# The first group's output projection as Strassen pairs: branches added in attention, one k pair's operands formed there, two up pairs' weights formed beside the queries

## The chip, the cores and the metric

The kernel runs on one NeuronCore of a Trainium2 chip. The metric is the device time of one execution in microseconds. In the views, PE is the tensor engine (PEld its weight loads), DVE the vector engine, ACT the scalar engine, POOL the GpSimd engine and SP the engine whose queue issues most DMAs.

## The reference

One layer of a decoder for 1024 prompt positions and 8 samples of 8 positions, D = 1024, all fp32. What matters here, for each group of tokens:

```python
q, k, v, gu, gv, ga, gb = split_in(rmsnorm(x, norm_mix) @ w_in)
o = sink_attention(q, k, v, ...)                # window of 128, 16 heads of 64
s = spatial_gating(gelu(gu), layernorm(gelu(gv)), ws, bs)
merged = sigmoid(ga) * (o @ w_pa) + sigmoid(gb) * (s @ w_pb)
x = x + merged @ w_out                          # the output projection
f, nconv = conv_ffn(rmsnorm(x, norm_ffn), w_up, conv_w, conv_b, w_down, conv_prev)
return rmsnorm(x + f), ...
```

`merged @ w_out` is 1088 tokens by 1024 by 1024. Also returned are the windows of keys and values, the last convolution rows and the normalised v rows of the samples.

## The kernel before

**Layout.** Activations are kept transposed: a tile holds 128 features on the partitions and tokens along the columns. D is KD = 8 such tiles. The tokens are two groups: group 0 has 576 columns (64 sample and 512 prompt tokens), group 1 has 512.

**Precision.** An fp32 product is made of three products in fp32r. `split` writes a high part with a cast on ACT and the remainder with a subtraction on DVE (L40, L41); a product of weights w and activations x is then `wh·xh + wh·xl + wl·xh`. So each weight tile and each operand costs a cast on ACT and a subtraction on DVE before PE can use it.

**Two kinds of product.** `mm3` (L239) is the ordinary one: for an output tile, 8 k tiles times 3 products, in two column chunks (320 and 256 for group 0). `Chain` makes two output tiles together from two halves of the columns by the Strassen-Winograd scheme: 7 products instead of 8, each of 4 k pairs times 3 matmuls of half a group's columns (288 or 256). Its weights are seven combinations, four of them sums on DVE (`Weights.total`, L178), each split by itself. Its operands are seven combinations per k pair: `combine` (L261 to L264) makes four of them with four DVE instructions of 288 columns, and `split` then runs over all seven. The results of the seven products are put together from PSUM: `keep` copies some to SBUF on ACT (L280 to L282), and additions on DVE and one subtraction on POOL combine them (`put`, L287).

**Weights.** `Weights` (object `W`) has a list of units, one for each split. `W.get(ahead, loads)` returns the next unit's pair of tiles, and emits the splits of `ahead` units and the loads of `loads` items beyond it. Raw weights have 4 buffers and split ones 4 slots.

**Order.** The program is written as one order of Python calls; each engine runs its own instructions in the order that a scheduler of the framework gives them, and waits on semaphores. SP's queue issues the DMAs in its order. Long stages take a list of small jobs between their products: `behind(at, j)` runs one after each product of the first Strassen stage, `fill` after each step of attention.

**Stages**, with the times of the profile: normalisation and the first projections (0 to 112 us), Strassen pairs for queries, keys, gates and the gated unit (to 462; the queries of both groups run from about 133 to 222), attention of group 0 with the branch products `branch` between its steps (465 to 585), attention of group 1 with group 0's merge between its steps (585 to 681), the rest of group 1's merge (to 715.3), the output projection of group 0 (to 766.9) and group 1 (to 813), the up projection with the convolution (to 1273), the down projection and the end.

**Merge.** `merge(g, c, to)` multiplies the attention's output by w_branch_attn for tile c and multiplies the result by the gate (L1099). For group 1 it adds the stored branch product too (L1101). For group 0 the gated product is stored to DRAM (`msd`). In the stage of group 1's merge, `hold` loads product and branch of group 0's tile c again, they are added (L1402), and `operand` splits the sum into a plain operand of 576 columns.

**Output projection.** Group 0's eight tiles are `mm3` products. The addition of x is made from PSUM (L1418), the result is stored to `x1d`, squared on ACT (L1421, L1427), and the squares are summed on POOL (L1428).

**Up pairs formed early.** For the first NPRE = 2 pairs of up tiles, `pair_load`, `pair_unit` and `store` form the seven units from raw weights (sums at L1376), split them and store high and low parts to DRAM (`upd`). They are 16 steps: 4 run in group 1's merge, 12 in the output projection of group 0. The up projection loads them later as ready weights.

## Time and profile before

| | |
|---|---|
| Runs | 1518.04, 1520.92, 1520.64 us; median 1520.64 us |
| Profiled execution | 1520.02 us, span 1518.1 us, granted clock 0.997 |
| Query stage, 133 to 222 us | 89.0 us |
| Attention of group 1, 585 to 681 us | 96 us |
| Rest of group 1's merge | 681.0 to 715.3 us |
| Output projection of group 0 | 715.3 to 766.9 us |
| Output projection of group 1 | 766.9 to 813.0 us |

In a row of the window table each engine has its busy time in the window and the number of its instructions; PEclk is the granted clock of the tensor engine as a share of full speed. In a timeline a row is one instruction: start, duration, engine, line, operation, names of output and inputs, shapes, and in brackets how long the engine had been idle and what released it. Matmuls overlap, so their price is the distance of their starts and not their duration. A row of the waits reads: engine, name and line of the waiting instruction, what it waited for, total us, times, longest. A group of equal instructions has its busy time and mean ns behind the bar, and then the idle time of the engine before them.

### The profile page before, as it was taken

To read this page: it belongs to the slowest core of one execution; us is meant where nothing else is said; L and a number is where in the kernel's file an instruction comes from. 1 tells how busy PE (TensorE), PEld (TensorE's weight loads), DVE (VectorE), ACT (ScalarE), POOL (GpSimd) and SP (SyncE) were. 2 spreads that over 40 slices of the span, in tenths; PEclk is the share of its full clock that TensorE was granted. 3 is DMA by queue.
4 is the path that set the end of the run, shared out by engine and by line. 5 is a ranking of instruction groups with operands and counts; after the bars stand their busy time and mean duration, and the time that the engine had idled before them with its cause. 6 is when DMAs were issued, how large, how long until landed. Compare 5 with 4: busy or idle time off the path is not lost.

```text
span 1518.1 us, 31397 instructions
## 1 busy us (share of the span) xinstructions
PE 1499.2 (99%) x12194; PEld 1485.4 (98%) x12194; DVE 1158.3 (76%) x1903; ACT 823.3 (54%) x1751; POOL 264.5 (17%) x422
## 2 busy tenths in 40 slices
PE   9999999999999999999999999999999999999998
PEld 9999999999998999999999999999999999999997
DVE  6896778756645895989668888898898888785685
ACT  6655764454543774864444555555555556353463
POOL 0000012200120231330232222232142122000002
PEclk9999999999999999999999999999999999999998
DMA  8553457747759847748988333332332317973353
GB/s 283 165 182 111 178 180 252 233 135 260 241 187 317 269 159 224 235 165 301 338 280 280 128 109 126 114 119 106 107 126 106 107 58 245 361 234 96 117 187 132
DMA packets 137509, 286.70 MB, mean 189 GB/s; under 512 B 15249, under 2 KB 44369, under 8 KB 137361
## 3 DMA queue, kind: packets, MB, share of 16 engines
q1 hardware_dynamic: 132352, 279.85, 55.1%
q10 hardware_dynamic: 5008, 4.85, 0.9%
q8 instruction: 96, 1.57, 0.4%
q14 instruction: 53, 0.43, 0.1%
HBM read 195.76 MB, written 90.85 MB: 189 GB/s over the span
## 4 chain that ended last, share of the span: by engine, by line
PE 68%; DVE 5%; DMA 4%; issue 3%; ACT 2%; SPq 1%; POOL 1%; POOLq 0%; ACTq 0%; DVEq 0%
PE st L299 39%; PE dn L1739 13%; PE mm L239 10%; PE sc L1232 1%; PE pt L1265 1%; ACT s L1255 1%; PE mx L841 1%; DVE wl L41 1%; PE po L1293 1%; DMA sg1d<-z 1%; DMA q<-qd 1%; DMA upd<-hl 0%; DMA s<-sd 0%; POOL x L1800 0%; DMA stg<-mbd 0%
## 5 line engine op out<-in xcount | busy, mean ns | idle before, releaser
L299 PE MATMUL st<-th,wh 128*128 128x256 f32 (+1 forms) x2128 | 610.4, 287 | 2.5 <-ACT k L280 2.3
L299 PE MATMUL st<-tl,wh 128*128 128x256 f32 (+1 forms) x2128 | 608.5, 286 | 0.0
L299 PE MATMUL st<-th,wl 128*128 128x256 f32 (+1 forms) x2128 | 608.1, 286 | 0.0
L299 PEld LDWEIGHTS st<-th,wh 128*128 128x128 f32 x2128 | 400.0, 188 | 4.1 <-ACT k L280 3.4
L299 PEld LDWEIGHTS st<-th,wl 128*128 128x128 f32 x2128 | 400.2, 188 | 0.0
L299 PEld LDWEIGHTS st<-tl,wh 128*128 128x128 f32 x2128 | 399.7, 188 | 0.0
L41 DVE TENSOR_TENSOR wl<-wraw,wh 128x512 fp32r<-128x512 f32 (+2 forms) x204 | 158.8, 791 | 35.3 <-ACT wh L40 33.4
L40 ACT CAST wh<-wraw 128x512 fp32r<-128x512 f32 (+2 forms) x204 | 139.2, 694 | 82.2 <-PE st L299 33.2
L1739 PE MATMUL dn<-th,wh 128*128 128x288 f32 (+1 forms) x616 | 177.3, 288 | 0.0
L1739 PE MATMUL dn<-tl,wh 128*128 128x288 f32 (+1 forms) x616 | 176.8, 287 | 0.0
L1739 PE MATMUL dn<-th,wl 128*128 128x288 f32 (+1 forms) x616 | 176.7, 287 | 0.0
L40 ACT CAST wh<-ws 128x512 fp32r<-128x512 f32 x160 | 98.2, 622 | 101.6 <-PE st L299 63.9
L41 DVE TENSOR_TENSOR wl<-ws,wh 128x512 fp32r<-128x512 f32 x160 | 111.1, 707 | 45.3 <-ACT wh L40 43.3
L1739 PEld LDWEIGHTS dn<-th,wh 128*128 128x128 f32 x616 | 116.7, 190 | 0.0
L1739 PEld LDWEIGHTS dn<-tl,wh 128*128 128x128 f32 x616 | 115.6, 188 | 0.0
L1739 PEld LDWEIGHTS dn<-th,wl 128*128 128x128 f32 x616 | 115.6, 188 | 0.0
L287 POOL TENSOR_TENSOR z<-kn,k 128x256 f32<-128x256 f32 (+1 forms) x32 | 29.6, 931 | 307.5 <-ACT kn L282 290.2
L40 ACT CAST th<-traw 128x544 fp32r<-128x544 f32 (+1 forms) x85 | 54.1, 643 | 52.8 <-PE dn L1739 40.0
L41 DVE TENSOR_TENSOR tl<-traw,th 128x544 fp32r<-128x544 f32 (+1 forms) x85 | 61.4, 730 | 22.9 <-ACT th L40 22.8
L239 PE MATMUL mm<-s,wh 128*128 128x256 f32 (+1 forms) x384 | 76.4, 294 | 0.0
L530 PE MATMUL st<-w2h,th 128*128 128x256 f32 x308 | 74.3, 282 | 0.8 <-ACT w2h L40 0.8
L239 PE MATMUL mm<-ol,wh 128*128 128x256 f32 (+1 forms) x256 | 73.6, 288 | 0.4 <-DVE ol L41 0.4
(298 smaller groups left out, 3156.1 us busy)
## 6 DMA issues: line engine op xcount, KB each, us to landing
wraw<-wt SPq DMA_DIRECT2D x133, 512.0 KB
traw<-td SPq DMA_DIRECT2D x77, 272.0 KB
td<-za SPq DMA_DIRECT2D x22, 544.0 KB
wraw<-wt SPq DMA_DIRECT2D x35, 256.0 KB
upd<-hl SPq DMA_DIRECT2D x14, 512.0 KB
td<-t SPq DMA_DIRECT2D x11, 544.0 KB
qd<-q SPq DMA_DIRECT2D x8, 576.0 KB
q<-qd SPq DMA_DIRECT2D x8, 576.0 KB
```

Source lines behind the costliest of these rows:

```text
L40: S.copy(hi, src)
L41: V.tensor_sub(lo, src, hi.bitcast(F32))
L239: PE.matmul(ps[:, lo:lo + c1 - c0], u[:, k, :], v[:, c0:c1], start=(clear and k == 0 and i == 0), stop=(k == nk - 1 and i == 2), skip_grou ...
L287: op(to, pick(x, to, lo, hi), pick(y, to, lo, hi))
L299: PE.matmul(ps, u[:, kk, :], v, start=first and kk + i == 0, stop=kk == 3 and i == 2, skip_group_check=True)
L530: PE.matmul(ps, u, v[:, k, :], start=k + i == 0, stop=k == KD - 1 and i == 2)
L841: PE.matmul(ps[:, P * i:P * i + P], vn[:, i], late["wst"][:, c, :], start=True, stop=True)
L1232: PE.matmul(ps[:, h, o0:256], q, kst[kv][:, e, k0:cur + P], start=e == 0, stop=e == 1)
L1255: S.activation(s[:, h], s[:, h], AF.Exp, bias=nm[:, h:h + 1], accum_out=dn[:, h:h + 1])
L1265: PE.transpose(pt[:, h * P:h * P + P], s[:, h, 0:P], ident)
L1293: PE.matmul(half(po, e), v[:, b - 1 + e], half(x, e), start=e == 0 and x is ph, stop=False, skip_group_check=True)
L1739: PE.matmul(place(m, e), u[:, m, :], v[:, lo:hi], start=new and i + k == 0 and (e == 0 or m % 2 == 0), stop=i == NU - 1 and k == 2, skip_g ...
```

## The change

**Group 0's output projection is made of four Strassen pairs** (tiles p and p + 4) by a new class `Out(Chain)`: 4 x 7 products of 12 matmuls of 288 columns in place of eight `mm3` tiles. The results are added straight into the two tiles of x: four half tiles per pair by POOL from `keep`'s copies (L1488, L1491), three by DVE from PSUM (L1494). `x1_out` stores, squares and sums as before (POOL's sum is L1477). The weights are units of pairs, with sums and seven splits of 512 in place of two splits of 1024. PSUM has four banks for these products (`psw`), which the output projection of group 1 uses as well.

**The merge of group 0** adds the branch at once, like group 1's (L1147 in both cases), so the eight branches are loaded during the merge of group 0. It runs in the order 0, 4, 1, 5, 2, 6, 3, 7, and tiles 0 and 4 are not stored but kept: they make k pair 0, whose sums and splits run inside attention of group 1. The other six are stored to `msd`, loaded again in the stage of group 1's merge and formed there as k pairs 1 to 3 (`form_sums`, `form_first`, `form_rest`), in place of the loads, additions and plain splits of eight tiles.

**The two up pairs' units** are formed by `up_units`: 16 steps with other loads (12 of 256 KB in place of 4 of 512 KB), the same 14 splits and stores. They run in `behind`, after every second product from the second pair on, beside the queries.

The diff, cut to its core:

```diff
-            for at in (PA0, PA0, WO0, WO0):
-                for c in range(8):
-                    W.add(wt(at + c), KD)
+            for c in (*crossed, *range(8)):
+                W.add(wt(PA0 + c), KD)
+            for c in range(4):
+                W.add_pair(wt(WO0 + c), wt(WO0 + c + 4))
+            for c in range(8):
+                W.add(wt(WO0 + c), KD)
...
+                def step(f, j, x, add, drop):
+                    def go():
+                        if hold:
+                            nc.sync.dma_start(*hold.pop())
+                        if loads:
+                            load(*loads.pop(0))
+                        src = q[x][0]
+                        if add:
+                            V.tensor_add(src, src, q["y"][0])
+                        t = pool.tile([P, 2, 4, P], F32R, name="phl", bufs=2)
+                        split(t[:, 0], t[:, 1], src)
+                        hold.append((upd[f][j], t.bitcast(F32)))
...
             def behind(at, j):
 
+                if ahead and at > 0 and (7 * at + j) % 2 == 0:
+                    with tc.issue_after(W.last.ins), tc.issue_after(W.did[0].ins), tc.issue_after(W.did[1].ins):
+                        ahead.pop(0)()
...
                             V.tensor_mul(st["t"], st["t"], st["ps"][:, base:base + n])
-                            if g:
-                                V.tensor_add(st["t"], st["t"], st["u"])
+                            V.tensor_add(st["t"], st["t"], st["u"])
                             to(c, st["t"])
...
-            keep = lambda c, t: nc.sync.dma_start(msd[c], t)
+            def keep(c, t):
+                if c % 4:
+                    nc.sync.dma_start(msd[c], t)
+                else:
+                    held[c] = t
+                    if c:
+                        form_sums(0, tma, 1)
+                        form_first(0, tma)
+                        form_rest(0)
...
-                    if at == 1:
-                        t, u = held.pop(c)
-                        V.tensor_add(t, t, u)
-                        operand(0)(c, t)
-                        hold(c + 2)
+                    if kk < 4 and at == 0:
+                        if c % 2 == 0:
+                            form_sums(kk, hbp, 2)
+                        else:
+                            form_rest(kk)
                     go()
-                    if at == 2 and c % 2:
-                        ahead.pop(0)()
+                    if kk < 4 and at == 1 and c % 2 == 0:
+                        form_first(kk, tm0)
+                        hold(c + 6)
+                        hold(c + 7)
...
+            class Out(Chain):
+
+                def product(self, j, w):
+                    ps, (xc, xd), n2 = self.multiply(j, w), self.places, self.n2
+                    c0, c1, d0, d1 = (x[:, n2 * h:n2 * h + n2] for x in (xc, xd) for h in range(2))
+                    kept = self.kept
+                    if j in (0, 1, 2):
+                        name, to, op = (("1", c0, G.tensor_add), ("5", d1, G.tensor_sub), ("u", c1, G.tensor_add))[j]
+                        self.keep(name, ps)
+                        op(to, to, kept[name])
+                    elif j == 4:
+                        self.keep("n", ps)
+                        G.tensor_sub(d1, d1, kept["n"])
+                    else:
+                        to, op = {3: (c1, V.tensor_add), 5: (c0, V.tensor_add), 6: (d0, V.tensor_sub)}[j]
+                        op(to, to, ps)
...
-            for c in range(KD):
-                xt = x_next(0, c)
-                w, ps = W.get(), acc2()
-                mm3(ps, groups[0]["chunks"], w, ms[0], 0, KD, KD)
-                for _ in range(1 + c % 2):
-                    ahead.pop(0)()
-                x1_tile(groups[0], c, ps, xt)
+            for p in range(4):
+                xc, xd = xs
+                chain = Out(0, tx, psw, xsp, (xc, xd))
+                for j in range(7):
+                    chain.product(j, W.get(3, 1))
+                    if j == 1 and p < 3:
+                        xs = [x_of(groups[0], c) for c in (p + 1, p + 5)]
+                    if j == 5:
+                        x1_out(0, p, xc)
+                x1_out(0, p + 4, xd)
```

How DVE's order changes late in the attention of group 1, around the end of a block (`of`, `ol` are the block's output, `pl` the low part of its transposed probabilities, `s` the scores, `stg` a merged tile, `wl` the low part of a weight tile). Before:

```order
L1304 TENSOR_TENSOR of_8900<-po_8891,ot_8898 64x256
L41 TENSOR_TENSOR pl_8911<-pt_8905,ph_8910 128x512
L1099 TENSOR_TENSOR stg_8955<-stg_8955,mm_8963 128x576
L41 TENSOR_TENSOR ol2_8576<-of_8900,oh2_8575 128x2x128
L1257 RECIPROCAL dn_8919<-dn_8919 128x4
L41 TENSOR_TENSOR wl_9365<-wraw_9151,wh_9364 128x1024
L1258 TENSOR_TENSOR s_8885<-s_8885,dn_8919 128x4x128
```

Now, at the block with the corresponding merge:

```order
L1350 TENSOR_TENSOR of_8959<-po_8950,ot_8957 64x256 x2
L40 TENSOR_TENSOR pl_8901<-pt_8895,ph_8900 128x512
L1147 TENSOR_TENSOR stg_8858<-stg_8858,stg_8860 128x576
L1303 RECIPROCAL dn_8909<-dn_8909 128x4
L1304 TENSOR_TENSOR s_8852<-s_8852,dn_8909 128x4x128
L1288 COPY_PREDICATED s_8932<-c_mprev_473,sc_8916 128x4x128
L40 TENSOR_TENSOR ol2_8696<-of_8959,oh2_8695 128x2x128
```

The addition of the branch, L1147, now stands between the probabilities' split and the softmax product, and the block's output split stands behind both.

DVE in the output projection of group 0 (`ml7` is the last merge operand, `hl` an up pair's unit, `wl` the low part of this projection's weights, `stg` a tile of x). Before, from the last merge operand on:

```order
L41 TENSOR_TENSOR ml7_9884<-stg_9811,mh7_9883 128x512
L41 TENSOR_TENSOR hl_10020<-ra_9414,hl_10020 128x512
L1418 TENSOR_TENSOR stg_9888<-stg_9888,mm_9898 128x576
L41 TENSOR_TENSOR wl_10099<-wraw_9958,wh_10098 128x1024
L41 TENSOR_TENSOR hl_10086<-rb_9416,hl_10086 128x512
L1418 TENSOR_TENSOR stg_9890<-stg_9890,mm_9964 128x576
L41 TENSOR_TENSOR wl_10169<-wraw_10030,wh_10168 128x1024
L1418 TENSOR_TENSOR stg_9956<-stg_9956,mm_10036 128x576
```

Now, most of the first pair (`ws` is a sum of weights, `st` a bank of PSUM; the names of raw tiles differ only by their buffers):

```order
L177 TENSOR_TENSOR ws_10149<-ws_10122,wraw_9921 128x512
L40 TENSOR_TENSOR wl_10101<-ws_10122,wh_10100 128x512
L177 TENSOR_TENSOR ws_10169<-wraw_9921,wraw_9923 128x512
L1494 TENSOR_TENSOR stg_10003<-stg_10003,st_10029 128x288
L40 TENSOR_TENSOR wl_10148<-ws_10149,wh_10147 128x512
L40 TENSOR_TENSOR wl_10148<-ws_10169,wh_10147 128x512
L177 TENSOR_TENSOR ws_10246<-wraw_10145 128x512
L177 TENSOR_TENSOR ws_10270<-ws_10246,wraw_10143 128x512
L1494 TENSOR_TENSOR stg_10003<-stg_10003,st_10106 128x288
L40 TENSOR_TENSOR wl_10194<-wraw_9921,wh_10193 128x512
L40 TENSOR_TENSOR wl_10194<-wraw_9923,wh_10193 128x512
L1494 TENSOR_TENSOR stg_10005<-stg_10005,st_10007 128x288
```

The additions L1494 from PSUM are shorter and stand among sums and splits of the weights; the up pairs' splits are gone from here.

POOL in the same stage (`rs0` is the sum of squares). Before, one addition for each tile but the first:

```order
L1428 TENSOR_TENSOR rs0_216<-rs0_216,stg_10025 128x576
L1428 TENSOR_TENSOR rs0_216<-rs0_216,stg_10091 128x576
L1428 TENSOR_TENSOR rs0_216<-rs0_216,stg_10161 128x576
L1428 TENSOR_TENSOR rs0_216<-rs0_216,stg_10229 128x576
L1428 TENSOR_TENSOR rs0_216<-rs0_216,stg_10303 128x576
```

Now, the first pair and part of the second:

```order
L1488 TENSOR_TENSOR stg_10003<-stg_10003,k1_10020 128x288
L1488 TENSOR_TENSOR stg_10005<-stg_10005,k5_10042 128x288
L1488 TENSOR_TENSOR stg_10003<-stg_10003,ku_10063 128x288
L1491 TENSOR_TENSOR stg_10005<-stg_10005,kn_10097 128x288
L1477 TENSOR_TENSOR rs0_216<-rs0_216,sq_10140 128x576
L1488 TENSOR_TENSOR stg_10045<-stg_10045,k1_10166 128x288
```

Four additions into the tiles of x precede the square's addition in each pair.

More of the change, by code (lines that the diff above doesn't have):

```diff
@@ L403, in dest256 @@
                 return ready, go
+            crossed = [c + 4 * e for c in range(4) for e in range(2)]
             blocks = {"gv0": GV0, "gv1": GV0 + 2, "gv2": GV0 + 4, "v": V0}
@@ L991, in layer @@
                 if at == 6:
+                    while ahead:
+                        ahead.pop(0)()
                     qko.close()
@@ L1382, in store @@
-            def store():
-                if "store" in pair:
-                    nc.sync.dma_start(*pair.pop("store"))
-            held = {}
-            def hold(c):
-                if c < KD:
-                    held[c] = [pwp.tile([P, 576], F32, name=x, bufs=3) for x in "mb"]
-                    for x, src in zip(held[c], (msd[c], mbd[0][c])):
-                        nc.sync.dma_start(x, src)
-            hold(0)
-            hold(1)
-            ahead = [x for f in range(NPRE) for x in (pair_load(f), *(pair_unit(f, j) for j in range(7)))]
@@ L1397, in layer @@
[L1397 to L1407 removed]
+            pso.close()
@@ L1421, in x1_tile @@
                     S.activation(nacc, x, AF.Square)
[L1422 removed]
+                elif g and c == KD - 1:
                     late["sq"] = traw()[:, :n]
```

147 lines of the change are left out of this document (85 added, 62 removed).

## The prediction

> **What bounds the kernel now.** I read the page first, for the engines' shares.
>
> ```profile
> span 1518.1 us, 31397 instructions
> PE 1499.2 (99%) x12194; PEld 1485.4 (98%) x12194; DVE 1158.3 (76%) x1903; ACT 823.3 (54%) x1751; POOL 264.5 (17%) x422
> ```
>
> The matmul engine works in 99% of the span. A change can gain only by giving it fewer or shorter matmuls, and it loses wherever the matmuls come to wait. The profiled execution took 1520.0 us, 1.9 us more than its span and 0.6 us less than the median of the runs, 1520.64, whose spread is 2.9 us; I sum against 1520.0. The share of DVE, 76%, is a mean over stages, so the second view is the table of busy time by window: the query stage (133 to 222 us), the opening and the middle of the second attention (595 to 672), the rest of the second group's merge (681 to 715), the first group's output projection (to 767) and the first of the up projection.
>
> ```profile
> core 0: us, PE busy (x) PEld busy (x) DVE busy (x) ACT busy (x) POOL busy (x), PEclk, DMA share, GB/s
> 133.00:222.00 89.00, 89.00 (x720) 89.00 (x720) 63.31 (x98) 59.87 (x121) 6.89 (x8) 1.00 0.46 161
> 595.00:606.00 11.00, 11.00 (x87) 10.59 (x86) 8.73 (x14) 7.50 (x26) 2.50 (x8) 1.00 1.08 288
> 606.00:672.00 66.00, 65.73 (x513) 63.57 (x512) 62.18 (x117) 52.95 (x166) 27.08 (x65) 1.00 0.64 204
> 681.00:715.30 34.30, 34.30 (x305) 34.30 (x305) 32.60 (x47) 17.35 (x24) 0.00 (x0) 1.00 0.84 284
> 715.30:766.90 51.60, 51.30 (x390) 51.13 (x389) 32.23 (x39) 20.41 (x29) 10.83 (x8) 1.00 0.94 329
> 813.00:850.00 37.00, 36.91 (x282) 36.71 (x282) 32.44 (x69) 20.16 (x45) 7.05 (x8) 1.00 0.65 228
> ```
>
> PE never rests for long, and the granted clock (PEclk) is full. What differs is DVE: 63.3 of 89 us in the query stage, 62.2 of 66 in the middle of attention, 32.2 of 51.6 in the output projection. So the output projection is bound by matmuls alone, with 19 us of DVE to spare, and attention is the stage in which work handed to DVE has 3.8 us of room. The waits from 681 to 767 us and one piece of the chain say the same:
>
> ```profile
> ACT hl L40 <- DMA upd<-hl: 8.7, 4, 4.2
> PE mm L239 <- DVE stg L1418: 0.3, 1, 0.3
> 718.82 7.39 DMA upd<-hl
> ```
>
> PE waits there once, 0.3 us, for the addition L1418. Behind that stands the store of the up pairs' weights: the casts of the next ones waited 8.7 us for it, and the chain passes through it. After the change those stores are made some 500 us earlier.
>
> **Output projection of the first group, matmuls.** Before, each of the 8 tiles takes 8 k tiles of 3 products in two chunks, 320 and 256 columns: 192 matmuls of each width. The timeline of PE at the stage's first and last matmuls:
>
> ```profile
> 715.29 0.30 PE L239 MATMUL mm<-mh,wh 128*128 128x320 f32 x1
> 715.43 0.31 PE L239 MATMUL mm<-ml,wh 128*128 128x320 f32 x1
> 765.78 0.28 PE L239 MATMUL mm<-mh,wh 128*128 128x256 f32 x1
> 765.90 0.28 PE L239 MATMUL mm<-ml,wh 128*128 128x256 f32 x1
> ```
>
> Records overlap, so the price is the distance of starts, 0.14 to 0.15 and 0.12 us. The stage itself, 51.6 us by its window, holds 192 x 0.147 + 192 x 0.118 = 50.9 and the 0.3 of waiting. After it come 4 pairs x 7 products x 4 k pairs x 3 = 336 matmuls of 288 columns. Such matmuls run in the up projection; the timeline there, two rows ten matmuls apart, and the groups of the window 829 to 846:
>
> ```profile
> 835.83 0.29 PE L299 MATMUL st<-tl,wh 128*128 128x288 f32 x1
> ...
> 837.16 0.29 PE L299 MATMUL st<-th,wl 128*128 128x288 f32 x1
> ...
> L299 PE MATMUL st<-th,wl 128*128 128x288 f32 x44 | 12.9, 294 | 0.0
> L299 PE MATMUL st<-tl,wh 128*128 128x288 f32 x43 | 12.7, 295 | 0.0
> L299 PE MATMUL st<-th,wh 128*128 128x288 f32 x43 | 12.7, 295 | 0.0
> ```
>
> Ten starts in 1.33 us are 0.133; 130 matmuls in 17 us are 0.131. At 0.132 the stage takes 336 x 0.132 = 44.4 us: 51.6 - 44.4 = **7.2 us less**, if nothing stalls. That term is counts by pitches and I hold it for certain.
>
> **The same stage on DVE and POOL.** DVE's price is also a distance of starts. The timeline at 681 us:
>
> ```profile
> 681.38 0.69 DVE L1099 TENSOR_TENSOR stg<-stg,mm 128x512 f32<-128x512 f32 x1 [0.94 <-PE mm L239]
> 681.98 0.75 DVE L1402 TENSOR_TENSOR m<-m,b 128x576 f32<-128x576 f32 x1
> 682.65 0.68 DVE L1101 TENSOR_TENSOR stg<-stg 128x512 f32<-128x512 f32 x1
> ```
>
> So 512 columns cost 0.60 us and 576 cost 0.67; a record reads 0.08 more. A pair's weights need 4 sums and 7 splits of 512: 11 x 0.60 = 6.6 us. Three half tiles of 288 are added from PSUM, at 288/512 of 0.60 some 0.35 each, 1.1 together. That is 7.7 of the pair's 84 x 0.132 = 11.1 us, so DVE alone fits. POOL gets four additions of half a tile (L1488, L1491) and two of the squares (L1477) per pair. Their prices, by POOL's and DVE's timeline near 847 us and the group of the squares:
>
> ```profile
> 824.46 0.81 POOL L287 TENSOR_TENSOR zb<-kn,k 128x288 f32<-128x288 f32 x1 [6.90 <-ACT kn L282]
> 846.93 2.64 POOL L287 TENSOR_TENSOR zb<-kn,k 128x288 f32<-128x288 f32 x1 [5.03 <-ACT kn L282]
> ...
> 847.61 0.68 DVE L178 TENSOR_TENSOR ws<-ws,wraw 128x512 f32<-128x512 f32 x1
> 848.22 0.68 DVE L41 TENSOR_TENSOR wl<-ws,wh 128x512 fp32r<-128x512 f32 x1
> 848.82 0.51 DVE L287 TENSOR_TENSOR za<-k,st 128x64 f32<-128x64 f32 x2
> 849.25 0.87 DVE L41 TENSOR_TENSOR wl<-ws,wh 128x512 fp32r<-128x512 f32 x1
> ...
> L1428 POOL TENSOR_TENSOR rs<-rs,stg x7: 1491/1611/2134, 731.8 to 768.3; 128x576 f32<-128x576 f32 x7
> ```
>
> The same addition takes 0.81 us where DVE leaves it alone and 2.64 where DVE runs sums and splits back to back. It ends at 849.57, after DVE's addition from PSUM at 848.82, and the DVE split that starts beside its end takes 0.87 instead of 0.68. So the two engines do delay one another. Per pair POOL needs 4 x 0.81 + 2 x 1.49 = 6.2 us. The low end of what this costs PE is 0: three such additions lie in 813 to 850, where DVE is as dense, and PE lost 0.09 of 37 us. The high end is that the two never overlap: 6.6 + 6.2 = 12.8 us for a pair of 11.1, so 4 x 1.7 = 6.8 us. DVE's waits for PE and its additions from PSUM leave openings, 4.5 us in each pair; I take a third, **2.3 us more**.
>
> The Trainium skill, page "SBUF — State Buffer", section "Who interferes with whom", says that a DVE instruction with two SBUF inputs and a GpSimd instruction that reads SBUF exclude one another for their whole length, while a DVE instruction with at most one SBUF input does not. By that rule this term would be the high end and the forecast some 4.5 us later. The 2.64 us row agrees with it, the 0.09 us that PE lost does not yet decide.
>
> **Second attention.** Each of the 8 merges of the first group now adds its branch there (L1147): 8 x 0.67 = 5.4 us on DVE. The first k pair's operands are formed there too. The groups of the same work, done for the up projection between 772 and 850 us:
>
> ```profile
> L41 DVE TENSOR_TENSOR tl<-t,th 128x1152 fp32r<-128x1152 f32 x4 | 5.4, 1351 | 0.0
> L41 DVE TENSOR_TENSOR tl<-x,th 128x576 fp32r<-128x576 f32 x4 | 3.0, 749 | 0.0
> L261 DVE TENSOR_TENSOR t<-x 128x288 f32<-128x288 f32 x4 | 2.9, 718 | 0.0
> L264 DVE SCALAR_TENSOR_TENSOR t<-t,x 128x288 f32<-128x288 f32 x4 | 1.8, 449 | 0.0
> L41 DVE TENSOR_TENSOR tl<-x,th 128x288 fp32r<-128x288 f32 x4 | 1.8, 448 | 0.0
> ```
>
> One k pair: two sums at 0.72, two at 0.45, splits of 0.45, 0.75 and 1.35, together 4.9, and 7 x 0.08 of overlap less: 4.3 us. Ends: 0, if DVE's room and PE's merge matmuls cover all; 5.4 + 4.3 = 9.7, if PE follows DVE throughout. The forming and one addition (5.0) fall into the opening, where DVE had 11.0 - 8.7 = 2.3 us free: 2.7 more. Six additions (4.0) fall into the middle, where it had 3.8 of 66: I charge half, 2.0, since DVE's idle time there comes in pieces too short to hold them. The last addition of the eight lies before the opening. By the order of instructions ten more matmuls stand ahead of attention's last product, which lets them cover what was uncovered: 10 x 0.12 = 1.2 back. Sum **3.5 us more**. Behind a DVE that is late here stand the softmax products of the next block, and for those the transposes on PE wait.
>
> **Rest of the second merge.** DVE loses 16 operations of 576 (8 additions L1402, 8 splits: 10.7 us) and the share of the up pairs' weights, some 3.0. It gains three formings (12.9) and the first output pair's weights instead of two full splits (4.2). That is 3.4 more on 32.6 of 34.3 us, 1.7 beyond the window. Ends 0 and 1.7; I take 0, because the first products need only the first slices of the operands and because the second group's splits, which DVE runs last, are not needed for another 44 us.
>
> **Query stage.** 16 steps bring 8 sums and 14 splits of 512: DVE 22 x 0.60 = 13.2 us, ACT 14 casts at the 0.62 of this row:
>
> ```profile
> L40 ACT CAST wh<-ws 128x512 fp32r<-128x512 f32 x160 | 98.2, 622 | 101.6 <-PE st L299 63.9
> ```
>
> or 8.7 us. DVE rises from 63.3 to 76.5 of 89 us, ACT from 59.9 to 68.6. On the queue of SP 12 loads of 256 KB and 14 stores of 512 KB join, 10.5 MB: 118 GB/s on 161, below the 329 that the output projection moved. Each store is issued a step after its split, so that it should not hold up the weight loads behind it. Cover: the weights are formed three units ahead. At 94% DVE the middle of attention cost PE 0.27 of 66 us; so 0 to 0.3, I take **0.2 more**.
>
> **Sum.** 1520.0 - 7.2 + 2.3 + 3.5 + 0.2 = **1518.8 us**.
>
> **Rivals.** *A, the cover holds everywhere.* PE lost almost nothing in any window above, even at 94% DVE; then only the matmuls and the 0.2 count: 1520.0 - 7.2 + 0.2 = 1513.0. Against it stands attention's opening, whose room is half of what is added.
>
> *B, slower: DVE and POOL take turns in the output projection.* If every POOL operation shuts DVE out and DVE, in order, stands at an addition that POOL's result or a PSUM bank must precede, a pair costs 6.6 + 1.1 + 6.2 = 13.9 us instead of 11.1: 4 x 2.8 = 11.2 on the stage, more than the 7.2 saved. With attention's 3.5 and the 0.2: 1520.0 - 7.2 + 11.2 + 3.7 = 1527.7. It decides from where less than 2.8 us of POOL's 6.2 in a pair falls beside DVE's waits and its additions from PSUM; it turns the sum against the change when the stage loses over 3.5 us. For it speaks the 2.64 us row, against it that products end in four PSUM banks, so that PE can run ahead of both. The skill's rule named above, with each engine's work merely in sequence, lies between this and the forecast: 6.8 for 2.3, 1523.3.
>
> *C, attention pays in full*, 9.7 for 3.5: 1525.0. For it: DVE at 94%, in order. Against it: DVE feeds PE one block late, and merge matmuls stand between.
>
> **How the numbers follow.** Forecast, with its own range of 1516 to 1522: 0.47. A 0.25, B 0.17 (the exclusive turns without standing included), C 0.11. The range is 1512.5 to 1525.4: it holds the forecast, C and most of A, and leaves out B and the lower tail of A, 2 in 10. About 0.2%, 3.0 us, is what a measurement of this kernel can tell, so faster is below 1517.6 and slower above 1523.7. Faster: all of A and 0.12 of the forecast, 0.37. Slower: B and half of C, 0.22. Within: 0.41.
>
> **What would show it.** Right: 336 matmuls of 288 columns over 44 to 47 us, with PE's waits there for the weights' splits or for PSUM under 3 us; POOL's L1488 between 0.8 and 2.7 us; the second attention 2 to 5 us longer, with more waits of the transposes for DVE's L1304; the query stage as long as before; no waiting for upd stores after 700 us. Wrong: an output projection over 50 us (B); an attention as long as before (A) or 9 us longer (C); lost PE time in the query stage, or a stall between the second merge and the first product, which I put at nothing.

## The result and the profile after

The changed kernel takes 1531.7 us (median of 6 runs, 1529.69 to 1533.54) where the kernel before takes 1521.08 (6 runs, 1518.04 to 1523.39) in the same comparison: a ratio of 1.0069, 95% interval 1.0055 to 1.0083. It is 0.7% slower, where a change within 0.2% was forecast as the likeliest. The profiled execution took 1529.69 us. Its page:

```profile
span 1528.0 us, 31437 instructions
PE 1499.4 (98%) x12146; PEld 1481.2 (97%) x12146; DVE 1189.5 (78%) x1963; ACT 839.8 (55%) x1791; POOL 287.5 (19%) x438
```

There are 48 matmuls fewer and a span 9.9 us longer, so PE waits more. Where, the starts of PE's instructions tell. The table gives for both profiled executions the stretches between landmarks on PE: Q from the first Strassen product to the first branch product, B from there to the first merge product, A from there to the first product of the output projection (the second attention and the rest of its merge), O to the last product of the output projections, U the up projection, D the down projection to the final sums.

| us | Q | B | A | O | U | D |
|---|---|---|---|---|---|---|
| before | 348.0 | 120.4 | 134.7 | 97.4 | 460.5 | 188.6 |
| after | 353.0 | 119.2 | 146.1 | 93.9 | 460.5 | 185.6 |
| difference | +5.0 | -1.2 | +11.4 | -3.5 | 0.0 | -3.0 |

The 1.2 us of B are what Q's last wait gives back, so Q and B together lose 3.8. With 1.1 us that the first landmark comes late (112.2 to 113.3; between 111.6 and 113.5 over all kernels below), the sum is +9.8. Only O gained, and by half of what its matmuls should give; the attention lost 11.4. The windows of the changed kernel that answer to those before:

```profile
core 0: us, PE busy (x) PEld busy (x) DVE busy (x) ACT busy (x) POOL busy (x), PEclk, DMA share, GB/s
137.00:231.00 94.00, 91.78 (x726) 90.30 (x725) 77.44 (x121) 67.44 (x135) 9.29 (x9) 1.00 0.77 275
599.90:610.90 11.00, 10.45 (x80) 9.98 (x78) 11.00 (x19) 8.70 (x24) 3.25 (x5) 1.00 1.10 282
610.90:688.00 77.10, 70.01 (x523) 65.50 (x524) 66.08 (x126) 53.94 (x172) 31.65 (x68) 1.00 0.61 188
697.60:731.80 34.20, 34.20 (x290) 34.20 (x291) 34.16 (x55) 16.78 (x26) 0.00 (x0) 1.00 0.60 184
731.80:779.70 47.90, 45.69 (x338) 44.74 (x337) 40.63 (x51) 25.62 (x49) 27.43 (x23) 1.00 0.60 200
```

In the middle of the attention (610.9 to 688) PE is idle for 7.1 of 77.1 us, where it was idle for 0.3 of 66 before. But DVE is idle for 11.0 us there, more than the 3.8 before. A stage in which both engines wait is not bound by either; it is a chain that passes through both. PE's waits in that stretch (589.9 to 731.8) name its end:

```profile
PE po L1342 <- POOL c L1322: 6.3, 10, 1.1
PE po L1339 <- DVE of L1350: 0.9, 1, 0.9
PE sc L1278 <- DMA q<-qd: 0.2, 1, 0.2
PE mm L238 <- DVE stg L1146: 0.2, 1, 0.2
```

A block's product with the values (`po`) waits for POOL's masked copies (`c`), ten times. Before, it never did. The wait that was forecast, transposes for DVE's softmax product, is not in the list. One block in the changed kernel's timeline, the rows of its chain:

```profile
623.29 0.60 PE L1311 MATMUL pt<-c_ident,s 128*128 128x128 f32 x4
...
624.37 0.59 ACT L40 CAST ph<-pt 128x512 fp32r<-128x512 f32 x1
...
625.06 0.69 DVE L40 TENSOR_TENSOR pl<-pt,ph 128x512 fp32r<-128x512 f32 x1 [1.55 <-ACT ph L40]
...
625.98 1.76 POOL L1322 TENSOR_SCALAR_AFFINE_SELECT c<-pl 64x256 fp32r<-64x256 f32 x2
...
627.31 0.38 PE L1342 MATMUL po<-c,dvst 128*128 128x256 f32 x1 [0.89 <-POOL c L1322]
```

Transposes, cast, subtraction, two selects, product: 4.0 us, all of one block, and PE has to find something to do in between. In the kernel before this chain ran beside another block's work, as the order of its PE instructions shows. There, `pt_8462` is transposed, and the `po` that follows multiplies `ph_8405`, a block earlier; the block's own `ph_8467` comes only behind the next transposes:

```
L1265 MATMUL pt_8462<-c_ident_97,s_8368 128x128 x4
...
L1293 MATMUL po_8519<-ph_8405,vst_8205 128x4x64
...
L1265 MATMUL pt_8533<-c_ident_97,s_8430 128x128 x4
...
L1293 MATMUL po_8611<-ph_8467,vst_8205 128x4x64
```

In the changed kernel the product with `ph_8584`, which is the cast of `pt_8579`, follows that block's own transposes:

```
L1311 MATMUL pt_8579<-c_ident_97,s_8485 128x128 x4
...
L1339 MATMUL po_8731<-ph_8584,vst_8319 128x4x64
```

The Python text of the attention is the same in both. The scheduler has put the transposes one block later against the products, and the one-block distance that hid the chain is gone. It is so for all 16 blocks of the second attention.

### The profile page after: what moved, and what is told of

It is laid out like the page before. It is cut to its first block, busy times and chain, and to the rows that moved or that the text cites. A ratio compares the mean times of both kernels' runs of the same rounds, so it can differ in the third digit from the quotient of the medians.

```text
span 1528.0 us, 31437 instructions
## 1 busy us (share of the span) xinstructions
PE 1499.4 (98%) x12146; PEld 1481.2 (97%) x12146; DVE 1189.5 (78%) x1963; ACT 839.8 (55%) x1791; POOL 287.5 (19%) x438
## 4 chain that ended last, share of the span: by engine, by line
PE 65%; DVE 5%; DMA 4%; issue 3%; ACT 3%; POOL 2%; SPq 1%; POOLq 0%; ACTq 0%; DVEq 0%
PE st L298 41%; PE dn L1806 13%; PE mm L238 5%; PE st L238 3%; POOL c L1322 1%; DVE wl L40 1%; ACT s L1301 1%; DMA q<-qd 1%; DMA dvst<-dvd 1%; PE mx L847 1%; PE pt L1311 1%; DMA sg1d<-z 1%; ACT ph L40 1%; PE sc L1278 1%; ACT wh L40 1%
## 5 line engine op out<-in xcount | busy, mean ns | idle before, releaser
L40 DVE TENSOR_TENSOR wl<-wraw,wh 128x512 fp32r<-128x512 f32 (+2 forms) x208 | 162.1, 793 | 38.3 <-ACT wh L40 36.6
L40 ACT CAST wh<-ws 128x512 fp32r<-128x512 f32 x176 | 108.2, 622 | 110.6 <-PE st L298 57.6
L40 DVE TENSOR_TENSOR wl<-ws,wh 128x512 fp32r<-128x512 f32 x176 | 125.8, 729 | 41.9 <-ACT wh L40 40.2
L279 ACT COPY k<-st 128x256 f32<-128x256 f32 (+1 forms) x160 | 58.8, 382 | 31.6 <-PE st L298 30.9
```

The lines of the kernel that those rows point to most:

```text
L40: return S.copy(hi, src), V.tensor_sub(lo, src, hi.bitcast(F32))
L279: S.copy(t, src)
```

## The experiments

The stretches of each kernel, as in the table above. The expectations of the first three speak of a stretch that begins a little later than A (4.4 us before, 4.2 after: 130.3 and 141.9 us). The ratios are to runs of the kernel before that were made beside each kernel's own; experiments 6, 9 and 12 have one run each.

| us | Q | B | A | O | U | D | ratio to before (95%) |
|---|---|---|---|---|---|---|---|
| before | 348.0 | 120.4 | 134.7 | 97.4 | 460.5 | 188.6 | |
| after | 353.0 | 119.2 | 146.1 | 93.9 | 460.5 | 185.6 | 1.0069 (1.0055 to 1.0083) |
| 1 no additions | 353.3 | 119.0 | 139.2 | 95.0 | 460.4 | 185.6 | 1.0043 (1.0029 to 1.0057) |
| 2 formed late | 354.5 | 119.1 | 138.2 | 97.1 | 460.4 | 185.6 | 1.0057 (1.0041 to 1.0074) |
| 3 order tied | 353.1 | 119.6 | 140.3 | 93.4 | 460.4 | 185.6 | 1.0035 (1.0021 to 1.0050) |
| 4 sums earlier | 352.0 | 119.4 | 145.9 | 93.9 | 460.5 | 188.6 | 1.0068 (1.0047 to 1.0089) |
| 5 no early pairs | 348.7 | 119.1 | 145.6 | 94.7 | 473.1 | 185.6 | 1.0131 (1.0110 to 1.0152) |
| 6 transfers only | 349.5 | 119.4 | 146.6 | 93.9 | 460.5 | 185.6 | one run, 1525.1 us to 1518.8 |
| 7 additions on DVE | 353.0 | 119.3 | 144.6 | 91.3 | 460.6 | 185.6 | 1.0051 (1.0030 to 1.0072) |
| 8 order, no early pairs | 349.7 | 119.9 | 138.6 | 94.9 | 472.4 | 188.5 | 1.0094 (1.0074 to 1.0114) |
| 9 order, no additions | 354.1 | 119.9 | 135.9 | 94.9 | 460.7 | 185.9 | one run, 1522.7 us to 1517.6 |
| 10 order, DVE, spread | 355.3 | 119.1 | 139.2 | 91.1 | 460.7 | 185.6 | 1.0035 (1.0022 to 1.0048) |
| 11 late, DVE, spread | 353.1 | 119.3 | 140.3 | 92.6 | 460.7 | 185.6 | 1.0040 (1.0026 to 1.0055) |
| 12 casts only | 350.9 | 119.1 | 145.4 | 94.9 | 460.5 | 185.6 | one run, 1526.3 us to 1522.3 |

My theory was O, that the order of PE costs the time in attention; its rival D, that DVE's added work does.

**1. No additions.**

```diff
-                            V.tensor_add(st["t"], st["t"], st["u"])
+                            if g:
+                                V.tensor_add(st["t"], st["t"], st["u"])
```

> The additions of the branch to group 0's merged tiles are left out (8 additions of 576 columns on DVE, 5.4 us, gone from the second attention); the branch of group 0 is thus missing from the sum. The order of PE keeps the changed kernel's pattern: each block's product with the values stands right behind the same block's transposes. From the first product of the second attention to the first product of the output projection the kernel before took 130.3 us and the changed one 141.9. Theory O (the order of PE exposes the chain transposes, cast, split, POOL's selects inside one block): still 139 to 142, waits of the products for POOL's c of over 4 us. Theory D (DVE has too much to do there): 5 to 6 us less, 135 to 137.

A fell by 6.9 us to 139.2, a little more than D expected; 1.5 of it is a pace of matmuls that has nothing to do with the additions (last section). PE's waits for `c` fell to 3.3 us, although the order kept the chain inside one block:

```profile
PE po L1343 <- POOL c L1323: 3.3, 6, 0.6
PE sc L1279 <- DMA q<-qd: 1.0, 1, 1.0
```

So O alone is wrong: the additions count. They count on the chain, too: POOL's selects from `pl` took 528 ns each instead of 624 (rows below).

**2. Formed late.** Tiles 0 and 4 are stored and loaded like the others, and all four k pairs are formed in the stage of the second merge.

```diff
-                if c % 4:
-                    nc.sync.dma_start(msd[c], t)
-                else:
...
+                nc.sync.dma_start(msd[c], t)
...
-                kk = c // 2 + 1
+                kk = c // 2
```

> The first k pair's operands are formed in the stage of the second merge like the other three, not at the opening of the second attention; the additions of the branch stay. With this the order of PE in the second attention is that of the kernel before: the product of a block stands behind the transposes of the next. Theory O: the stretch that took 130.3 us before and 141.9 in the changed kernel takes 131 to 134, and no product waits for POOL's c; the output projection may start 1 to 2 us late, since its operands come later. Theory D: DVE loses 4.3 us there, so 137 to 138.

A is 138.2, 7.9 us less; O is 3.2 more. The operands were expected to come late to the output projection, but PE doesn't wait for them: its waits there are for ACT's copies out of PSUM, 4.8 us where the changed kernel has 2.2. The order of PE is the former one, with a block between. No `po` waits for POOL, the transposes wait for DVE in its place:

```profile
PE pt L1311 <- DVE s L1304: 2.9, 3, 1.9
PE po L1339 <- ACT ph L40: 0.7, 1, 0.7
PE sc L1278 <- DMA q<-qd: 0.2, 1, 0.2
```

In the first experiment, with the additions gone, the order stayed as the change made it; here, with the forming gone, it is the former. So it is the forming at the opening of the attention that turned the order. That its cost is the order's, this kernel can't show, since DVE's work left with it.

**3. Order tied.** All work stays where the change put it.

```diff
                         for h in range(4):
-                            PE.transpose(pt[:, h * P:h * P + P], s[:, h, 0:P], ident)
+                            late["tr"] = PE.transpose(pt[:, h * P:h * P + P], s[:, h, 0:P], ident)
...
                         if i >= 3:
-                            pv_p(*steps[i - 3])
+                            with tc.issue_after(late["tr"].ins):
+                                pv_p(*steps[i - 3])
```

> All work as in the changed kernel, forming and additions in attention; only PE's order is tied: a block's product with the values is queued behind the transposes of the next block, as it stood before. Theory O: the stretch falls from 141.9 us to 131 to 135 and the waits of the products for POOL's c are gone. Theory D: DVE has as much to do as in the changed kernel, so nothing is gained, 140 to 143, or more if the transposes then wait for the softmax.

A is 140.3: 5.8 us less with not one instruction fewer. D gave nothing for that, so the order is a cause; O's range, 131 to 135 for the shorter stretch, is missed by 1 (some 136 with the 4.3 taken off), so it is not the whole. The longest waits of this kernel show a part of what is left:

```profile
PE pt L1311 <- DVE s L1304: 2.9, 2, 1.6
PE po L1339 <- ACT ph L40: 0.7, 1, 0.7
PE sc L1278 <- DMA q<-qd: 0.5, 1, 0.5
```

This is the wait that the prediction had named, transposes for DVE's softmax product.

**9. Order tied and no additions**, the third and the first together.

> The order of PE tied as in the third experiment, and the branch of group 0 left out of the sum as in the first: of the three things that the change put on the second attention only the forming of the first k pair is left. The stretch from the first merge product to the output projection took 134.7 us before, 146.1 in the changed kernel, 140.3 with the order tied, 139.2 without the additions. If order and load are separate, 135 to 137.5: what the additions cost is gone (4 or so) and the forming keeps 1 to 2. If without the additions the order costs nothing, it stays at 139.

A is 135.9, 1.2 above the kernel before. The theories were both half of it, and the two causes overlap: tying the order saves 5.8 us with the additions (146.1 to 140.3) and 3.3 without them (139.2 to 135.9). The 4.4 us that the third kernel still has above the ninth are not simply the additions' time on DVE. In the third, no merge matmul is left to run between the transposes and the products of the last two blocks of attention; 3.6 of its 4.5 us of waits lie there, and in the middle of them the granted clock falls to half, from 680.0 to 686.8 us:

```profile
676.00:680.00 4.00, 2.04 (x16) 1.65 (x16) 3.80 (x8) 2.22 (x7) 1.44 (x3) 1.00 0.52 167
680.00:684.00 4.00, 2.36 (x12) 2.05 (x12) 2.28 (x6) 2.32 (x9) 1.29 (x3) 0.50 0.72 263
684.00:688.00 4.00, 3.89 (x22) 3.56 (x22) 2.37 (x5) 1.52 (x5) 1.72 (x4) 0.65 0.00 0
```

PE worked in about 5.2 of those 6.8 us, so the half clock costs some 2.6 us (an estimate). In the ninth, 13 merge matmuls run behind the first of those transposes, and the clock in A is full. Another 1.5 us between the two is the pace of the last section. So the 11.4 us don't divide into shares that add up. The order costs A 3.3 us without the additions and 5.8 with them, each time between two profiles of the same pace. The additions cost some 5.4 where the chain lies open (the 6.9 of the first experiment less 1.5 of pace); what they cost where the order hides it stays open. So does the price of the forming: A is 138.2 and 140.3 us where the pair is formed late (2 and 11) and 138.6 to 140.3 where it is formed in attention with the order tied (3, 8 and 10), all five with a stretch of half clock in A.

Next the query stage. Theory Q1 was that ACT, in order, stands before casts of sums that DVE has not made, so that the copies out of PSUM come late; Q2 that DVE and ACT simply have more to do; Q3 that the transfers are in the way. ACT's longest kinds of wait that the steps bring, between 137 and 231 us of the changed kernel, and PE's two:

```profile
ACT phl L40 <- DVE stg L909: 6.7, 4, 2.7
...
ACT wh L40 <- DVE ws L177: 2.5, 3, 1.3
ACT phl L40 <- DMA upd<-phl: 2.4, 2, 2.1
ACT q L40 <- DMA kd<-q: 2.3, 1, 2.3
...
PE st L298 <- ACT ku L279: 1.2, 1, 1.2
PE st L298 <- ACT k L279: 1.0, 2, 0.6
```

**4. Sums earlier.**

```diff
                         src = q[x][0]
-                        if add:
-                            V.tensor_add(src, src, q["y"][0])
...
                         for name in drop:
                             q[name].pop(0)
+                        if not add or j == 4 and f + 1 < NPRE:
+                            total()
```

> The sums of the two up pairs' weights beside the queries are made at the end of the step before, so that the cast on ACT finds its sum ready. The query stage of the changed kernel lost 4.1 us between 183 and 226 us, in waits of PE for ACT's copies of products out of PSUM. Theory Q1 (ACT, in order, stands at the cast of a sum that DVE has not made, with those copies behind it): the loss falls to 1.5 us or less, the total by 2.5 to 4. Theory Q2 (DVE and ACT simply carry 22 and 14 instructions more): the loss stays at 3.5 to 4.5, the total as in the changed kernel.

Q fell by 1.0 us to 352.0 and the total by nothing that can be measured. Q1 falls. ACT's waits for the sums of the steps went from 6.7 to 1.7 us, but those for the sums of the other weights rose from 2.7 to 5.3 and those for stores of the steps from 2.4 to 5.3: other waits took the place of the one removed.

**5. No early pairs.** NPRE is 0, and `up_units` isn't called.

> No up pair is formed ahead at all: the 16 steps beside the queries are gone, and the first two up pairs are formed in the up projection like every other. The stretch from the first Strassen product to attention took 348.0 us before, 353.0 in the changed kernel. Both theories of the query stage expect 348 to 349 here, which would show that the steps are the cause and not anything else that moved; the up projection, 460.5 us in both kernels, shows what forming them there costs, 0 to 4 us.

Q is 348.7, so the steps are the cause of its loss. U is 473.1, 12.6 us more, three times what I allowed. At the start of the up projection DVE is busy without a break (11.93 of 12 us from 816 to 828), and PE's waits in U come to 7.6 us, 4.0 of them one wait for ACT's squares. In that wait the granted clock falls to half, from 824.9 to 835.2 us, and that is most of the rest. One window in it, and two of its starts:

```profile
828.00:832.00 4.00, 4.00 (x19) 4.00 (x19) 0.76 (x3) 0.00 (x0) 1.03 (x1) 0.50 0.51 158
831.08 0.44 PE L298 MATMUL st<-th,wl 128*128 128x288 f32 x1
831.32 0.44 PE L298 MATMUL st<-th,wh 128*128 128x288 f32 x1
```

The starts of matmuls of 288 columns are 0.24 us apart there, and 0.13 at full clock. Forming the pairs beside the queries costs about 4 us and saves 12.6.

**6. Transfers only.**

```diff
-                        if add:
-                            V.tensor_add(src, src, q["y"][0])
-                        t = pool.tile([P, 2, 4, P], F32R, name="phl", bufs=2)
-                        split(t[:, 0], t[:, 1], src)
-                        hold.append((upd[f][j], t.bitcast(F32)))
+                        for e in range(2):
+                            hold.append((upd[f][j][:, e], src))
```

> The steps beside the queries keep their loads and stores but neither sums nor splits: raw weights are stored as high and low part, so the first two up pairs multiply with wrong weights. Theory Q2 (load of DVE and ACT): the loss goes, 348 to 349.5 us. Theory Q3 (transfers: the 10.5 MB delay the stores of queries and keys, ACT stands before a buffer that such a store still reads, and the copies out of PSUM queue behind): 350.5 to 353.

Q is 349.5, and PE is busy for 94.00 of 94 us between 137 and 231 while the core moves as much as in the changed kernel (281 GB/s to 275). Q3 falls: transfers alone cost PE nothing here.

**12. Casts only**, the same with a tile for the cast, without sums and subtractions.

```diff
+                        t = pool.tile([P, 4, P], F32R, name="phl", bufs=2)
+                        S.copy(t, src)
                         for e in range(2):
-                            hold.append((upd[f][j][:, e], src))
+                            hold.append((upd[f][j][:, e], t.bitcast(F32)))
```

> The steps beside the queries keep loads, stores and ACT's 14 casts; DVE's 8 sums and 14 subtractions are left out, so the first two up pairs multiply with wrong weights. The stretch from the first Strassen product to attention took 348.0 us before, 353.0 in the changed kernel, 349.5 with transfers only. If ACT's casts alone push back the copies out of PSUM: 352 to 353. If it is DVE that is late, and ACT that stands before casts of sums and of other weights waiting for DVE: 349 to 350.5.

Q is 350.9, between the ranges, but what it lost lies behind the steps (two waits, at 255 and 264 us): in their window PE rests in this kernel as little as with transfers only.

```profile
137.00:231.00 94.00, 94.00 (x755) 93.62 (x754) 66.36 (x103) 70.05 (x140) 8.23 (x9) 1.00 0.80 278
```

ACT is busier here (70.05 us) than in the changed kernel (67.44), and DVE has 66.36 in place of 77.44. So most of the price of the steps is DVE's (what causes the two waits behind them isn't shown): 22 instructions more make it late for ACT's casts of sums and for the splits, and ACT, in order, makes the copies out of PSUM late, for which PE waits.

Last the output projection. In the changed kernel PE waits 2.2 us in the first group's stage, for ACT's copies out of PSUM.

**7. Additions on DVE.**

```diff
-                        name, to, op = (("1", c0, G.tensor_add), ("5", d1, G.tensor_sub), ("u", c1, G.tensor_add))[j]
+                        name, to, op = (("1", c0, V.tensor_add), ("5", d1, V.tensor_sub), ("u", c1, V.tensor_add))[j]
...
-                        G.tensor_sub(d1, d1, kept["n"])
+                        V.tensor_sub(d1, d1, kept["n"])
```

> The four additions per pair that POOL makes into the tiles of x in the first group's output projection are made by DVE, from the same copies. The stage takes 47.9 us in the changed kernel, 44.4 by its matmuls. Theory T (POOL and DVE shut one another out, so POOL's work stretches DVE's splits and with them ACT's): DVE's splits of 512 fall from 1.0 us to under 0.8, the stage to 44.4 to 46. Theory L (DVE is late by its own load): four more additions of 0.37 us a pair make it worse, 48 to 50.

The first group's stage, from its first product to that of the second group, takes 45.3 us; the changed kernel's took 47.9. DVE got 16 additions, and its busy time did not grow:

```profile
729.00:774.30 45.30, 44.93 (x338) 44.64 (x337) 40.59 (x69) 25.32 (x48) 7.70 (x7) 1.00 0.65 214
```

40.59 us for 69 instructions (two more fall into the window), where 51 instructions had taken 40.63. The groups say why. In the changed kernel, and then with the additions on DVE:

```profile
L40 DVE TENSOR_TENSOR wl<-ws,wh 128x512 fp32r<-128x512 f32 x12 | 11.7, 989 | 0.0
L177 DVE TENSOR_TENSOR ws<-ws,wraw 128x512 f32<-128x512 f32 x6 | 5.6, 936 | 0.2
L1494 DVE TENSOR_TENSOR stg<-stg,st 128x288 f32<-128x288 f32 x11 | 4.9, 447 | 0.7 <-POOL stg L1488 0.7
```

```profile
L40 DVE TENSOR_TENSOR wl<-ws,wh 128x512 fp32r<-128x512 f32 x13 | 8.8, 680 | 0.0
L1494 DVE TENSOR_TENSOR stg<-stg,st 128x288 f32<-128x288 f32 x11 | 4.9, 445 | 0.1
L177 DVE TENSOR_TENSOR ws<-ws,wraw 128x512 f32<-128x512 f32 x6 | 4.1, 681 | 0.0
```

The same splits take 989 and 680 ns, the sums 936 and 681. The additions from PSUM (L1494), with one input in SBUF, are not stretched: 447 and 445. What POOL was given cost DVE as much as if DVE had done it, and came late besides. Theory T holds, L falls. (The splits from raw weights have a mean of 957 ns in this kernel, where POOL still adds the squares: each takes 0.68 us, but for three beside such an addition, which take 1.58 to 1.91.)

**8. Order tied and no early pairs.**

> The tied order of PE in the second attention together with no early up pairs. If the two causes are separate, the gains add: query stage as in the kernel before, attention as in the kernel with the order tied; against the kernel before, the output projection's 3.7 us are kept, the attention gives back 4 to 5, the up projection pays as in the kernel without early pairs: 1518 to 1523 where the kernel before takes 1518 to 1521.

The gains add in Q and A (349.7 and 138.6), but U pays 11.9 as in the fifth, with the same 4.0 us of waiting and the same fall of the clock. My total was some 12 us too low, since it was worked out before the fifth experiment's U was known.

**10 and 11. A better version?** The third (10) or the second (11) with the seventh, and the steps begun earlier and farther apart:

```diff
-                if ahead and at > 0 and (7 * at + j) % 2 == 0:
+                if ahead and (7 * at + j) % 3 == 0:
```

> Three changes together: PE's order tied in the second attention, POOL's four additions per output pair on DVE, and the 16 steps beside the queries begun with the first pair and spread over every third product in place of every second. The gains should add: attention -6, output projection -2.6, and the query stage, whose loss is that of instructions packed too densely, 1 to 3 us less. Against the kernel before: the output projection keeps 6, attention gives back 5 to 6, the query stage 1 to 3: between 1 us faster and 3 us slower than before.

> As the run before, but the first k pair's operands are formed in the stage of the second merge, which gives the order of PE back without tying it. Attention costs some 2 us less than with the order tied, the start of the output projection 2 to 3 more, since the operands come later to it. Between 1 us faster and 4 us slower than the kernel before.

By their ratios, 1.0035 and 1.0040, both beat the changed kernel, the eleventh narrowly, and both are slower than the one before by 5 to 6 us, outside what I had allowed (3 and 4). In the tenth, A and O came out as the parts had. In the eleventh A didn't: 140.3 us is no less than with the order tied and 2.1 more than in the second, 1.5 of it the pace. The spreading failed, with Q at 355.3 and 353.1, no better than 353.0; in each of them 3.4 us of Q run at half clock, which costs some 1.6 us. In the tenth, where O gains 6.3 us (97.4 to 91.1), A gives back 4.5 and Q and B 6.0.

## Why the prediction was wrong

**Matmuls of the output projection, -7.2: right but for some 0.4.** With the additions on DVE the stage takes 45.3 us, 0.4 of it a wait of PE, where 44.4 was worked out. The stage before was read too long: by the starts it ran from 715.29 to 766.49, 51.2 us and not 51.6, which is also what the prediction's own 50.9 and 0.3 add up to.

**Stalls there, +2.3: mechanism right, size low.** The stage took 47.9, so 3.5. Of that 2.6 went with POOL's four additions (seventh experiment). It lies between the third that I took and the 6.8 of strict turns. By the rule of the Trainium skill, page "SBUF — State Buffer", section "Who interferes with whom", a DVE instruction with two SBUF inputs and a GpSimd one that reads SBUF exclude one another; the 989 and 680 ns of the same split agree with it. That exclusion doesn't become PE's loss one for one: DVE was busy for 40.6 of 47.9 us and had room.

**Second attention, +3.5: wrong, 11.4.** The step that failed is the one that took PE's order in attention as given. I counted that ten more matmuls stood ahead of attention's last product and booked them as a gain of 1.2; I did not look at which block's product stood behind which block's transposes. In rival C I even leaned on it, where "DVE feeds PE one block late" stands as the reason against: that distance was gone for every block. Tying it back gives 5.8 us, or 3.3 with the additions left out, and the wait that the turned order brings (`po` for `c`) is not in the trace of before, so no row of it could price it. Rival C, full payment for DVE's work, came near in size (9.7) by luck and not in kind. The rest, additions and forming with the order as before, measures 5.6 for 3.5 (140.3 to 134.7). By the estimates above some 2.6 of it is half clock behind waits at the end of attention, a term that the sum doesn't have, and 1.5 the pace of matmuls; how the remainder divides between additions and forming stays open.

**Rest of the second merge, 0: right as to waits.** PE is busy for 34.20 of 34.20 us with DVE at 34.16. Yet it made 290 matmuls there where it had made 305 in 34.30 us before: the slower pace of the last section, 1.5 us of A's 11.4.

**Query stage, +0.2: wrong, 3.8 with B.** The bound was the failing step. I took the middle of attention, where PE lost 0.27 of 66 us with DVE at 94%, as the worst that a busy DVE does. In attention merge matmuls with ready operands fill the gaps; in the query stage every product needs PSUM banks that ACT has to copy out, and ACT waits for DVE in its own order. At 77.4 of 94 us, 82%, DVE was already late for that. The transfers, which I had added up with more care, cost nothing that shows (sixth experiment).

**The rivals.** B's mechanism is there, at a quarter of its price (2.6 of 11.2). A was wrong on all three covers. The range, up to 1525.4, was too narrow because both of its ends were sums over waits that the trace of before could show.

## What to carry to other kernels

An instruction added ahead of a software pipeline can turn the order that a scheduler makes of it: compare, on the bound engine, which block's consumer stands behind which block's producer, before pricing anything. A busy share is a bound only for the stage it was measured in; ask of the new stage which in-order engine stands between the busy one and the bound one. Additions handed to POOL beside a DVE full of two-input work in SBUF saved DVE nothing here. And a wait of PE can cost more than its length: behind some of those here the granted clock fell to half for 3.4 to 10.2 us. Look at PEclk in the stretch behind a wait before dividing a loss among causes.

## What the runs showed of the hardware

**Half clock.** Apart from the first and the last 11 us of each kernel, the granted clock fell to 0.50 in stretches of 3.4, 6.8 or 10.2 us, each in or right behind waits of PE: at the end of attention in kernels 2, 3, 8, 10 and 11, at the start of U in 5 and 8, in Q in 10 and 11, at the start of B in 8 and 9. The kernel before and the changed one have none. The length of a single wait doesn't decide it: the sixth waits 1.9 us at 277 us and stays at full clock. What does stays open.

**Two paces.** The matmuls of 256 columns ran at two paces that don't follow the code of the stage. In the down projection they start every 0.117 to 0.118 us in the profiles of before, 4 and 8 (D is 188.5 to 188.6) and every 0.113 in the others (185.6 to 185.9), though kernels 5 and 8 have the same down projection and the granted clock is full in both. Two neighbouring starts of the kernel before, and two of the changed one:

```profile
1299.92 0.28 PE L1739 MATMUL dn<-tl,wh 128*128 128x256 f32 x1
1300.04 0.28 PE L1739 MATMUL dn<-th,wl 128*128 128x256 f32 x1
```

```profile
1312.11 0.28 PE L1806 MATMUL dn<-th,wl 128*128 128x256 f32 x1
1312.22 0.28 PE L1806 MATMUL dn<-th,wh 128*128 128x256 f32 x1
```

The 3.0 us of D in the first table are this, and no effect of the change. The last 34 us of A, the rest of the second merge, have the two paces too: 0.113 in before, 1, 2, 8, 9 and 10, 0.118 in the changed kernel, 3, 4, 6 and 11, and both in 5, 7 and 12. With some 290 matmuls there that is 1.5 us of A. What sets the pace stays open.

**POOL's select.** Its copies from `pl` took 508 ns before, 624 in the changed kernel and 528 with the additions left out.

```profile
L1276 POOL TENSOR_SCALAR_AFFINE_SELECT c<-pl 64x256 fp32r<-64x256 f32 x32 | 16.3, 508 | 4.7 <-DVE pl L41 3.3
```

```profile
L1322 POOL TENSOR_SCALAR_AFFINE_SELECT c<-pl 64x256 fp32r<-64x256 f32 x32 | 20.0, 624 | 2.3 <-DVE pl L40 0.3
```

```profile
L1323 POOL TENSOR_SCALAR_AFFINE_SELECT c<-pl 64x256 fp32r<-64x256 f32 x32 | 16.9, 528 | 2.2 <-DVE pl L40 0.2
```
